# Four pairs of query tiles ahead instead of six, with attention's loads on SyncE and the statistics in one tile

## The chip, the cores and the metric

The kernel runs on one core of a Trainium2 chip. The core has TensorE (PE: matrix products into PSUM), VectorE (DVE), ScalarE (ACT), GpSimd (POOL) and SyncE (SP), which only issues transfers. Each engine works through its own list of instructions in order; they meet through semaphores. Sixteen DMA engines move data for all of them. SyncE's transfers go through a hardware queue (q1 in the profile), GpSimd's through a software queue (q0). The metric is the device time of one execution in microseconds, as the median of the runs.

## The reference

The kernel computes a decoder trunk of two layers over 1024 tokens of width 1024, in float32.

- Layer A is gated linear attention with four heads: projections of `x`, a recurrence in chunks, a gate, an output projection, and a layer norm on `ALPHA * x + y`.
- Layer B is attention in dilated windows over one shared K and V. Three groups of windows (width 128 step 1, 512 step 4, 2048 step 16) have their own queries and keys. There are eight query heads and two key heads, so four query heads share a key head.

```python
q, g = jnp.split(x @ w_in, [SWA_Q_TOTAL], axis=-1)
q = rope(q...) * SWA_HEAD_DIM ** -0.5
for gi, (window, dilation) in enumerate(SWA_GROUPS):
    o_g, lse_g = dilated_window_attention(q[:, :, gi], k_sh[:, :, gi], v_sh[:, :, gi], window, dilation)
wts = jax.nn.softmax(jnp.stack(lses, axis=0), axis=0)
o = jnp.sum(wts[..., None] * jnp.stack(outs, axis=0), axis=0)
return (o * jax.nn.silu(g)) @ w_out
```

The three groups' results are weighted by a softmax over the groups' log-sums. So for every token and head the minimum (the kernel works with negated scores) and the sum of the exponentials of all three groups have to meet before the outputs can be added.

## The kernel before, in words

**Products.** A float32 product is made from three products in the faster format `float32r`: a matrix is split into a high part (`wh`, `xh`) and the rest (`wl`, `xl`), and high x high, high x rest and rest x high are added up in PSUM. `project` makes 128 columns of a projection for all 1024 tokens: two halves of 512 tokens, eight steps, three products each, which is 48 matmuls of 512 columns (`acc<-x1h,wh` and its like). `load_w_now` loads the weight into `wf` (two buffers). With `added=True` ScalarE writes `wh` and the negated weight into `wl` (three buffers of each), and a GpSimd transfer adds the weight from memory onto `wl`.

**Pairs ahead.** `seven` makes two projections at once by Strassen's scheme: seven products of quarters in place of eight, 7 x 4 x 3 = 84 matmuls (`sev<-...`). `load_pair` fetches both weights (on SyncE) and forms the sums of quarters. The first three pairs are the keys; six more are query tiles, listed in `EARLY` as (unit, unit, group). The tiles wait in memory (`kd`, `qd`).

**Attention.** A unit is one query head. For `u` from 0 to 7 the loop in `layer_b` records `scores(u)`, `q_proj(u + 1)`, `attend(u)` and, for the first four units, `g_proj(u)`; the other gates come behind the loop.

- `q_proj` fetches a tile that is in `qd`, and projects the others.
- `scores` forms the scores (`lv<-K,Q`) of the groups 2, 1 and 0. VectorE adds the mask and takes the minimum, ScalarE takes the exponential and its sum. Both go into `sts`. The three groups order the tokens differently, so the statistics of groups 1 and 0 go through memory: `std<-sts` writes them, `nat<-std` gathers them in the order of group 2. From these VectorE and ScalarE form the factors `ew`; those of groups 0 and 1 go through memory again (`cwd<-ew`, `cw<-cwd`). All these small transfers are on SyncE.
- `attend` scales the probabilities `P` with the factors, turns them (`ms<-ident,P`), and multiplies with V (`po<-diag,V` for group 2, `po<-PT,V` for the others).
- `g_proj` is one more projection, with a tanh, that multiplies the unit's result `og`.

K and V of one key head are fetched by `reload_k` and `reload_v`. The second head's follow at `u == 3`. Weights (`wf`, `wl`), Q, K and V of attention are all issued by GpSimd.

**What sets the order.** The kernel records its operations, and a list scheduler (`Sched.order`) places them one by one, by the earliest start under a cost for each operation and then by the recorded rank. `later` changes the rank, `landing` adds to a transfer's cost. In the cost of before SyncE's and GpSimd's transfers don't slow each other. What the scheduler puts out is the fixed order of each engine's list. All operations are issued in one line of the code, so the profile's rows all bear that line's number (L454) and are told apart by the tiles.

## Time and profile before

| what | value |
|---|---|
| median of three runs | 1165.43 us (1163.35 to 1167.08) |
| the profiled execution | 1165.53 us |
| its span, from the first to the last instruction | 1163.8 us |
| mean granted clock of TensorE | 0.994 |
| PE busy | 1134.9 us |
| DVE, ACT, POOL busy | 833.9, 588.3, 212.2 us |
| transfers by SyncE's queue | 100.84 MB, 28.0% of 16 engines' span |
| transfers by GpSimd's queue | 39.85 MB, 14.5% |

A row of the view by stretches has the stretch, its length, then for each engine the busy time and the number of instructions, the granted clock of TensorE (1.00 is full speed), the share of the span that the DMA engines were busy, and GB/s. A row of a timeline has the start, the duration, the engine, the line, the operation with the tile written and the tiles read, and in brackets how long the engine stood idle before it and what ended that. A row of the chain of waits has start, duration, and what was waited for. A float32 product counts as two records of the matrix engine, a `float32r` product as one. Matmuls overlap, so rates are read from the distance of their starts.

### The profile page before, as it was taken

How to read it: one execution, taken by the hardware profiler on the slowest of the kernel's cores; microseconds unless marked ns; L12 is line 12 of the kernel's file. 1: busy time of each engine (PE TensorE's matmuls, PEld its weight loads, DVE VectorE, ACT ScalarE, POOL GpSimd, SP SyncE). 2: the span in 40 equal slices, each digit the busy share in tenths (PEclk: the TensorE clock that was granted, in tenths of full speed). 3: DMA queues.
4: the chain of work that ended last, by engine and by line, in shares of the span. 5: the costliest groups of instructions: out<-in, count | busy, mean ns of one | idle time of the engine just before them, and what ended most of it. 6: DMA issues, size and time to landing. Idle time of an engine off the chain costs nothing.

```text
span 1163.8 us, 20037 instructions
## 1 busy us (share of the span) xinstructions
PE 1134.9 (98%) x7672; PEld 956.7 (82%) x7672; DVE 833.9 (72%) x1712; ACT 588.3 (51%) x1175; POOL 212.2 (18%) x216
## 2 busy tenths in 40 slices
PE   9999999999999999999999999999987999999997
PEld 9888888889887888888888887888876888787876
DVE  6286952786967699887988966757645767686678
ACT  5355531635563335655656556455444555553343
POOL 1000000101122120122222343212222222132200
PEclk9999999999999999999999999999998999999999
DMA  7111223121144454855564695353453433351645
GB/s 267 57 39 37 74 81 96 60 73 39 56 170 138 136 188 156 268 164 135 138 162 137 173 282 124 83 119 75 74 169 78 101 74 75 84 151 42 191 135 181
DMA packets 103744, 141.97 MB, mean 122 GB/s; under 512 B 45312, under 2 KB 61568, under 8 KB 103648
## 3 DMA queue, kind: packets, MB, share of 16 engines
q1 hardware_dynamic: 90592, 100.84, 28.0%
q0 software_dynamic: 13056, 39.85, 14.5%
q8 instruction: 60, 0.98, 0.4%
q14 instruction: 36, 0.29, 0.1%
HBM read 111.11 MB, written 29.56 MB: 121 GB/s over the span
## 4 chain that ended last, share of the span: by engine, by line
PE 66%; DVE 14%; DMA 11%; ACT 4%; issue 3%; SPq 1%; POOL 0%; DVEq 0%; ACTq 0%
PE acc L454 36%; PE po L454 8%; PE vac L454 7%; PE lv L454 6%; DMA wf<-in_wB 3%; PE ms L454 3%; PE sev L454 3%; PE pro L454 2%; DMA std<-sts 2%; DVE wl L454 2%; DVE rt L454 2%; DMA nat<-std 2%; DVE P L454 2%; DMA wf<-in_wOB 2%; DVE sum L454 2%
## 5 line engine op out<-in xcount | busy, mean ns | idle before, releaser
L454 ACT ACTIVATE wh<-wf 128x1024 fp32r<-128x1024 f32 (+3 forms) x113 | 105.8, 938 | 126.0 <-PE acc L454 89.7
L454 PE MATMUL acc<-x1h,wh 128*128 128x512 f32 x320 | 138.8, 434 | 0.8 <-ACT t L454 0.7
L454 PE MATMUL acc<-x1h,wl 128*128 128x512 f32 x320 | 126.1, 394 | 0.0
L454 PE MATMUL acc<-x1l,wh 128*128 128x512 f32 x320 | 125.7, 393 | 0.0
L454 ACT ACTIVATE P<-P,sts 128x128 f32<-128x128 f32 (+2 forms) x192 | 81.4, 425 | 84.8 <-DVE sts L454 84.0
L454 DVE TENSOR_TENSOR wl<-wf,wh 128x1024 fp32r<-128x1024 f32 (+3 forms) x61 | 76.9, 1260 | 44.6 <-ACT wh L454 34.2
L454 PE MATMUL acc<-xh,wh 128*128 128x512 f32 x256 | 102.0, 398 | 0.0
L454 PE MATMUL acc<-xh,wl 128*128 128x512 f32 x256 | 99.8, 390 | 0.0
L454 PE MATMUL acc<-xl,wh 128*128 128x512 f32 x256 | 99.7, 390 | 0.0
L454 PE MATMUL sev<-T,wh 128*128 128x512 f32 x288 | 89.6, 392 | 0.8 <-ACT wh L454 0.4
L454 PE MATMUL lv<-K,Q 128*64 128x64 f32 (+2 forms) x512 | 72.3, 295 | 5.2 <-DMA Q<-qd 3.0
L454 PEld LDWEIGHTS acc<-x1h,wl 128*128 128x128 f32 x320 | 60.6, 189 | 13.5
L454 PEld LDWEIGHTS acc<-x1h,wh 128*128 128x128 f32 x320 | 61.1, 191 | 11.7 <-ACT t L454 1.6
L454 PEld LDWEIGHTS acc<-x1l,wh 128*128 128x128 f32 x320 | 61.0, 191 | 10.3
L454 PEld LDWEIGHTS lv<-K,Q 128*128 128x128 f32 (+1 forms) x512 | 53.4, 169 | 17.5 <-DVE sts L454 5.3
L454 PEld LDWEIGHTS sev<-T,wh 128*128 128x128 f32 x288 | 53.5, 188 | 14.2 <-ACT u L454 2.2
L454 POOL TENSOR_TENSOR wl<-wf,wh 128x1024 fp32r<-128x1024 f32 x9 | 21.5, 2386 | 231.5 <-PE ms L454 145.4
L454 DVE CUSTOM_DVE_ANT_0 P<-lv,bmask 128x256 f32<-128x256 f32 (+1 forms) x128 | 45.5, 376 | 21.0 <-PE lv L454 20.6
L454 PE MATMUL acc<-ogh,wh 128*128 128x512 f32 x152 | 60.1, 396 | 0.1
L454 PE MATMUL acc<-ogl,wh 128*128 128x512 f32 x152 | 59.3, 390 | 0.2 <-POOL ogl L454 0.2
L454 PE MATMUL acc<-ogh,wl 128*128 128x512 f32 x152 | 59.2, 389 | 0.0
L454 PE MATMUL sev<-T,wl 128*128 128x512 f32 x144 | 56.3, 391 | 0.9 <-DVE wl L454 0.9
(305 smaller groups left out, 2908.9 us busy)
## 6 DMA issues: line engine op xcount, KB each, us to landing
wf<-in_wA SPq DMA_DIRECT2D x24, 512.0 KB
wf<-in_wB POOLq DMA_DIRECT2D x20, 512.0 KB, 4.9
wl<-in_wB POOLq DMA_DIRECT2D x20, 512.0 KB, 8.0
wf<-in_wO SPq DMA_DIRECT2D x16, 512.0 KB
wf<-in_wOB SPq DMA_DIRECT2D x16, 512.0 KB
wf<-in_wV SPq DMA_DIRECT2D x12, 512.0 KB
wf<-in_wB SPq DMA_DIRECT2D x12, 512.0 KB
qd<-pair SPq DMA_DIRECT2D x12, 512.0 KB
```

Of the source, the lines that this page charges most:

```text
L454: getattr(handle[o.eng], meth)(*[conv(a) for a in args], **{k: conv(v) for k, v in kw.items()})
```

## The change

- `EARLY` holds four pairs, all of group 2, and no longer the two of group 1. So every unit now projects its queries of groups 0 and 1 in attention; for units 0, 2, 4 and 6 that is one projection more.
- The loads of `wf`, Q, K and V move from GpSimd to SyncE. The addition onto `wl` stays on GpSimd.
- `behind` makes a transfer depend on whoever wrote a given tile. The second head's K and V are put behind the write of the fourth unit's factors, `cwd[3]`.
- The gate `g_proj(u - 1)` is recorded behind `scores(u)` for u from 1 to 4, where `g_proj(u)` stood behind `attend(u)`.
- The statistics of group 2 are written directly into a third row of `nat`, which gets two buffers as `ew` does. So two reductions over three rows replace the pairwise minima and sums, and the group's factors are read from `ew` without a copy.
- The scheduler's cost puts all transfers on one common resource; GpSimd's cost 1.7 times as much.

```diff
-QUEUED, ISSUE = 5.2, 0.9
-EARLY = [(0, 1, 2), (2, 3, 2), (0, 2, 1), (4, 5, 2), (6, 7, 2), (4, 6, 1)]
+QUEUED, ISSUE, ADDED = 2.4, 0.9, 1.7
+EARLY = [(0, 1, 2), (2, 3, 2), (4, 5, 2), (6, 7, 2)]
...
+        behind = [v for v in self.trail if meth == "dma_start"]
...
-        o.reads += ins
+        o.reads += ins + behind
...
             if o.calls[0][0] == "dma_start":
-                queue[e] = max(queue[e], st) + c
-                o.t1 = st + c + QUEUED if e == "POOL" else queue[e] + 1.7
-                free[e] = st + (ISSUE if e == "POOL" else 0.37)
+                added = e == "POOL"
+                dma_free = max(dma_free, st + ISSUE * added) + c * (ADDED if added else 1.0)
+                o.t1 = dma_free + (QUEUED if added else 1.7)
+                free[e] = st + (ISSUE if added else 0.37)
...
-        (S.gpsimd if added else S.sync).dma_start(wf, src)
+        S.sync.dma_start(wf, src)
...
-                S.gpsimd.dma_start(K[c][g], kd[c][g])
+                S.sync.dma_start(K[c][g], kd[c][g])
...
-                    S.gpsimd.dma_start(Q[g], qd[u, g])
+                    S.sync.dma_start(Q[g], qd[u, g])
...
-            sts = hp.tile([128, 2, 24], F32, name="sts", bufs=2)
+            sts = hp.tile([128, 2, 16], F32, name="sts", bufs=2)
+            nat = hp.tile([128, 2, 3, 8], F32, name="nat", bufs=2)
...
+                        least, mass = (nat[:, i, 2, j:j + 1] if g == 2 else sts[:, i, col:col + 1] for i in range(2))
...
-            S.vector.tensor_tensor(mn, nat[:, 0, 0, :], nat[:, 0, 1, :], op=OP.min)
-            S.vector.tensor_tensor(mn, mn, sts[:, 0, 16:24], op=OP.min)
-            ew = hp.tile([128, 3, 8], F32, name="ew", bufs=1)
-            S.vector.tensor_sub(ew[:, 0:2], mn[:, None, :].to_broadcast([128, 2, 8]), nat[:, 0])
-            S.vector.tensor_sub(ew[:, 2], mn, sts[:, 0, 16:24])
+            S.vector.tensor_reduce(out=mn, in_=nat[:, 0].rearrange("p g n -> p n g"), op=OP.min, axis=AX.X)
+            ew = hp.tile([128, 3, 8], F32, name="ew", bufs=2)
+            S.vector.tensor_sub(ew, mn[:, None, :].to_broadcast([128, 3, 8]), nat[:, 0])
             S.scalar.activation(ew, ew, AF.Exp)
-            zz = hp.tile([128, 3, 8], F32, name="zz", bufs=1)
-            S.vector.tensor_mul(zz[:, 0:2], ew[:, 0:2], nat[:, 1])
-            S.vector.tensor_mul(zz[:, 2], ew[:, 2], sts[:, 1, 16:24])
-            zs = hp.tile([128, 8], F32, name="zs", bufs=1)
-            S.vector.tensor_add(zs, zz[:, 0, :], zz[:, 1, :])
-            S.vector.tensor_add(zs, zs, zz[:, 2, :])
+            S.vector.tensor_mul(nat[:, 1], ew, nat[:, 1])
+            S.vector.tensor_reduce(out=zs, in_=nat[:, 1].rearrange("p g n -> p n g"), op=OP.add, axis=AX.X)
             S.vector.reciprocal(zs, zs)
             S.vector.tensor_mul(ew, ew, zs[:, None, :].to_broadcast([128, 3, 8]))
-            cw = hp.tile([128, 24], F32, name="cw", bufs=1)
-            S.vector.tensor_copy(cw[:, 16:24], ew[:, 2, :])
...
             scores(u)
+            if 0 < u < 5:
+                g_proj(u - 1)
             if u == 3:
-                reload_k(1)
+                with S.behind(cwd[3]):
+                    reload_k(1)
             if u + 1 < 8:
                 q_proj(u + 1)
             if u < 7:
                 attend(u)
-                if u < 4:
-                    g_proj(u)
             if u == 3:
-                reload_v(1)
+                with S.behind(cwd[3]):
+                    reload_v(1)
```

The diff shows the table `EARLY` and the recorded ranks; the order that follows from them is seen in the engines' lists. SyncE's list, at the fourth unit's statistics (`std3`, `nat`) and factors (`cwd3`, `cw`), up to the fifth unit's, before:

```order
L454 DMA std3_8333<-sts_8193 128x2x4 x2
L454 DMA nat_8357<-std3_8333 64x1x8 x4
L454 DMA std3_8333<-sts_8193 8x16x8 x2
L454 DMA nat_8357<-std3_8333 64x8x1 x4
L454 DMA cwd3_8541<-ew_8483 8x8x8 x4
L454 DMA cw_8538<-cwd3_8541 128x8x1
L454 DMA cw_8538<-cwd3_8541 128x2x4
L454 DMA std4_8740<-sts_8513 128x2x4 x2
```

And with the change (`K12` is the second head's K of group 2, `qd42` the fifth unit's queries of group 2, `V12` the second head's V):

```order
L462 DMA nat_7833<-std3_8048 64x8x1 x4
L462 DMA wf_8182<-in_wB 128x1024
L462 DMA cwd3_8209<-ew_8195 8x8x8 x4
L462 DMA cw_8193<-cwd3_8209 128x8x1
L462 DMA cw_8193<-cwd3_8209 128x2x4
L462 DMA K12_8254<-kd12_5828 128x1024
L462 DMA wf_8259<-in_wB 128x1024
L462 DMA K11_8266<-kd11_5638 128x1024
L462 DMA K10_8278<-kd10_5469 128x1024
L462 DMA Q_8283<-qd42_6321 128x1024
L462 DMA V12_8287<-vd31_4625 64x1x512 x2
L462 DMA V11_8292<-vd_4634 128x4x128
```

Weights, K, Q and V now stand in SyncE's list, K and V behind the factors, and the fifth unit's statistics behind these.

PE's list at the fifth unit's first scores (`lv<-K12,Q`), before:

```order
L454 MATMUL acc_8470<-x1l1_4298,wh_8124 128x512
L454 MATMUL acc_8470<-x1h1_4269,wl_8136 128x512
L454 MATMUL lv_8489<-K12_8383,Q_8420 64x64 x16
L454 MATMUL lv_8510<-K11_8395,Q_8412 128x128
L454 MATMUL acc_8470<-x1h2_4311,wh_8124 128x512
L454 MATMUL acc_8470<-x1l2_4325,wh_8124 128x512
```

And with the change:

```order
L462 MATMUL po_8379<-PT_8393,V00_6526 128x128
L462 MATMUL po_8379<-PT_8415,V00_6526 128x128
L462 MATMUL lv_8442<-K12_8254,Q_8283 64x64 x16
L462 MATMUL lv_8461<-K11_8266,Q_8309 128x128
L462 MATMUL acc_8372<-x1h4_4366,wh_8069 128x512
L462 MATMUL acc_8372<-x1l4_4377,wh_8069 128x512
```

Before, the fifth unit's scores stood inside a query projection and ahead of the fourth unit's `attend`; now they stand behind the whole of it, and the projection around is a gate's.

More of the change, by code (lines that the diff above doesn't have):

```diff
@@ L14 @@
 OP = mybir.AluOpType
+AX = mybir.AxisListType
 T = 1024
@@ L216, in landing, with behind @@
         return _Landing(self, us)
+    def behind(self, *views):
+        return _Behind(self, views)
     def depend(self):
@@ L282, in order @@
         done = []
-        queue = {e: 0.0 for e in self.ENG}
+        dma_free = 0.0
         cur_set = None
@@ L503, in __exit__, with __init__, __enter__ @@
         self.s.least = 0.0
+class _Behind:
+    def __init__(self, s, views):
+        self.s, self.views = s, list(views)
+    def __enter__(self):
+        self.s.trail = self.views
+    def __exit__(self, *a):
+        self.s.trail = []
 class _Landing:
@@ L1403, in reload_v @@
             V[c][0] = page(p0, F32, f"V{c}0")
-            S.gpsimd.dma_start(V[c][0], vd0[c])
+            S.sync.dma_start(V[c][0], vd0[c])
         reload_k(0)
@@ L1483, in scores @@
                             out=px, in0=sc[:, o:o + nk], in1=mk, scale=-QSCALE, scalar=-LOWEST,
-                            op0=OP.add, op1=OP.min, accum_out=sts[:, 0, col:col + 1])
-                        S.scalar.activation(px, px, AF.Exp, scale=-1.0, bias=sts[:, 0, col:col + 1],
-                                             accum_out=sts[:, 1, col:col + 1])
+                            op0=OP.add, op1=OP.min, accum_out=least)
+                        S.scalar.activation(px, px, AF.Exp, scale=-1.0, bias=least, accum_out=mass)
                         o += nk
@@ L1495, in scores @@
             dst = std[u]
-            nat = hp.tile([128, 2, 2, 8], F32, name="nat", bufs=1)
             with S.landing(RUNS):
@@ L1511, in scores @@
                                           dst[0, s].rearrange("(i b p) -> i p b", i=2, b=8)[i])
[L1512 to L1524 removed]
+            cw = hp.tile([128, 16], F32, name="cw", bufs=1)
+            mn, zs = cw[:, 0:8], cw[:, 8:16]
+            S.vector.tensor_reduce(out=mn, in_=nat[:, 0].rearrange("p g n -> p n g"), op=OP.min, axis=AX.X)
+            ew = hp.tile([128, 3, 8], F32, name="ew", bufs=2)
+            S.vector.tensor_sub(ew, mn[:, None, :].to_broadcast([128, 3, 8]), nat[:, 0])
+            S.scalar.activation(ew, ew, AF.Exp)
+            S.vector.tensor_mul(nat[:, 1], ew, nat[:, 1])
+            S.vector.tensor_reduce(out=zs, in_=nat[:, 1].rearrange("p g n -> p n g"), op=OP.add, axis=AX.X)
             S.vector.reciprocal(zs, zs)
             S.vector.tensor_mul(ew, ew, zs[:, None, :].to_broadcast([128, 3, 8]))
[L1527 to L1528 removed]
             with S.landing(RUNS):
@@ L1537, in scores @@
                                   cwd[u][1].rearrange("(n p r) -> p n r", n=2, r=4))
-            U[u]["cw"] = cw
+            U[u]["cw"], U[u]["ew"] = cw, ew
         def attend(u):
@@ L1566, in attend @@
             x = P[2, 0][0].rearrange("p (j k q) -> p k j q", j=4, k=2)
-            w = cw[:, 16:24].rearrange("p (k j one) -> p k j one", k=2, j=4)
+            w = U[u]["ew"][:, 2].rearrange("p (k j one) -> p k j one", k=2, j=4)
             S.vector.tensor_mul(x, x, w.to_broadcast([128, 2, 4, 64]))
```

6 lines of the change are left out of this document (3 added, 3 removed).

## The prediction

> **What bounds the kernel now.** I read the shares of the engines first, then the engines' busy time in six stretches that I cut at the kernel's stages: layer A, the pairs of tiles ahead, attention's first three units with the scores of the fourth, the thirty microseconds after these, the rest of attention, and the output with its layer norm.
>
> ```profile
> span 1163.8 us, 20037 instructions
> PE 1134.9 (98%) x7672; PEld 956.7 (82%) x7672; DVE 833.9 (72%) x1712; ACT 588.3 (51%) x1175; POOL 212.2 (18%) x216
> core 0: us, PE busy (x) PEld busy (x) DVE busy (x) ACT busy (x) POOL busy (x), PEclk, DMA share, GB/s
> 0.00:510.00 510.00, 507.20 (x4327) 433.44 (x4328) 366.37 (x558) 246.65 (x355) 57.17 (x38) 1.00 0.35 115
> 510.00:682.00 172.00, 170.65 (x741) 138.33 (x741) 143.03 (x198) 102.54 (x173) 49.07 (x51) 1.00 0.60 161
> 682.00:860.00 178.00, 175.68 (x1030) 148.04 (x1030) 118.91 (x397) 99.84 (x286) 45.70 (x63) 1.00 0.47 109
> 860.00:890.00 30.00, 19.82 (x110) 16.34 (x109) 7.09 (x36) 8.20 (x27) 6.41 (x10) 0.83 0.68 186
> 890.00:1081.00 191.00, 186.34 (x1120) 158.23 (x1119) 136.34 (x433) 101.67 (x294) 47.91 (x52) 1.00 0.35 82
> 1081.00:1163.00 82.00, 75.18 (x351) 62.27 (x350) 62.20 (x94) 29.44 (x42) 5.92 (x3) 0.99 0.55 180
> ```
>
> TensorE sets the time: it is busy in every stretch but one. Attention (682 to 1081) leaves 2.3 + 10.2 + 4.7 = 17.2 us of it idle, and 10.2 of these lie in 30 us, at a granted clock of 0.83. PE's timeline and the chain of waits show that place, between the fourth unit's last scores and its turned probabilities:
>
> ```profile
> 857.65 1.02 PE L454 MATMUL lv<-K,Q 128*128 128x256 f32 x4
> 870.57 2.64 PE L454 MATMUL lv<-K,Q 128*64 128x64 f32 x34 [3.01 <-DMA Q<-qd]
> 883.63 1.08 PE L454 MATMUL ms<-ident,P 128*128 128x128 f32 x4 [7.17 <-DVE sts L454]
> ...
> 860.23 11.54 DMA std<-sts
> 873.12 8.22 DMA nat<-std
> ...
> 959.15 1.81 DMA std<-sts
> 962.31 5.12 DMA nat<-std
> ...
> 855.60 1.91 POOL L454 DMA_DIRECT2D K<-kd  x3
> 860.00:870.00 10.00, 7.56 (x34) 5.91 (x32) 1.13 (x2) 3.09 (x4) 2.36 (x4) 1.00 0.96 316
> ```
>
> Two waits, 3.01 and 7.17 us, have one cause: GpSimd issues the second head's K (855.60) and V just ahead of the fourth unit's statistics. The DMA engines are 96% busy, and the round trip of the statistics takes 11.54 + 8.22 = 19.8 us; in the sixth unit it takes 1.81 + 5.12 = 6.9 us. VectorE stands in order behind the late statistics, so PE's next evacuations wait too.
>
> The idle time is not the whole price. After it PE starts at a low clock:
>
> ```profile
> 884.37 0.78 PE L454 MATMUL acc<-x1h,wh 128*128 128x512 f32 x1
> 888.09 1.95 PE L454 MATMUL po<-diag,V 128*128 128x128 f32 x16
> 880.00:890.00 10.00, 6.37 (x30) 5.64 (x31) 4.68 (x28) 4.52 (x20) 0.00 (x0) 0.66 0.18 33
> 872.87 0.77 PE L454 MATMUL acc<-x1h,wh 128*128 128x512 f32 x1
> 920.33 1.50 PE lv L454 x34
> 682.47 16.32 PE acc L454 x72
> ```
>
> A 512-column matmul takes 16.32 / 72 = 0.2267 us warm. The nine from 884.37 to 888.09 took 3.72 where 2.04 is normal: 1.7 lost. The 34 score records from 870.57 to 872.87 took 2.30 where the sixth unit's take 1.50: 0.8 lost. The matmuls just behind them I put at 0.5. So this place costs 10.2 + 3.0 = **13.2 us**.
>
> **The change part by part.**
>
> *Two pairs fewer.* A pair by seven products is 7 x 4 x 3 = 84 matmuls, 19.0 us; two go, and four plain projections of 48 come, 10.9 us each, into attention. PE's order counts 756 rows of the pairs' product before and 588 after, 960 rows of projection before and 1152 after: 24 more, 24 x 0.2267 = **+5.4 us**. Nothing hides this, since the stretch of the pairs is 99% busy. ScalarE's and VectorE's share of the work moves along into attention, where they are busy 210 and 262 of 399 us; there is room.
>
> *K and V behind the fourth unit's factors.* K, Q and V now leave SyncE after the write of `cwd[3]`, so nothing large but weights can cross that unit's statistics. SyncE holds behind these waits only work of later units. What is late next? The fifth unit's scores. From the first turned tile of unit four to these PE has 36 projection matmuls (8.2 us), eight `po<-diag` (1.8), 16 turns and 27 `po<-PT`, at about 0.11 us a record and two records each (3.5 + 6.0): about 19 us. K in three parts, a weight and Q are 2.5 MB; at the 316 GB/s of the row above 8 us, at worst the 15 us that passed from 855.60 to 870.57. The factors' four writes take 2.5 us to issue and land some 3 us later:
>
> ```profile
> 882.58 2.48 SPq L454 DMA_DIRECT2D cwd<-ew  x4
> 1058.67 3.08 DMA cwd<-ew
> ```
>
>  So it needs 13 to 20 us, of 19 and the lead that the next part gives: a wait of 0 to 3 us; I take under 1, as no statistics or V go along now.
>
> *Gates one unit later, two projections for every unit.* What PE has between a unit's last score and its own turn is now, by PE's order, 54, 81, 72, 75, 63, 60, 57 and 72 projection matmuls, and the next unit's scores: 14 to 24 us, shortest in the first (14.8) and the fifth unit (14.3). What the statistics need, from the units where PE waited at the end of it:
>
> ```profile
> 808.38 0.59 PE L454 MATMUL lv<-K,Q 128*128 128x256 f32 x2
> 822.63 0.63 PE L454 MATMUL ms<-ident,P 128*128 128x128 f32 x4 [0.69 <-DVE P L454]
> 957.34 0.61 PE L454 MATMUL lv<-K,Q 128*128 128x256 f32 x2
> 969.63 0.66 PE L454 MATMUL ms<-ident,P 128*128 128x128 f32 x4 [0.35 <-DVE P L454]
> 1042.23 0.59 PE L454 MATMUL lv<-K,Q 128*128 128x256 f32 x2
> 1059.13 0.63 PE L454 MATMUL ms<-ident,P 128*128 128x128 f32 x4 [0.61 <-DVE P L454]
> ```
>
> 13.7, 11.7 and, in the last unit, where VectorE has the output's splits to do as well, 16.3 us. The fourth unit has 17.0 where it had 13.5, so its 13.2 us go, unless the two reasons below bring part back.
>
> *Loads from GpSimd to SyncE.* Weights, Q, K and V now stand in SyncE's queue among the statistics, each issue about 0.35 us there, and a weight's issue waits for ScalarE to free its buffer. By the order that buffer was freed a projection earlier at every unit, so this wait should be over. A 512 KB load ahead of a small transfer costs it 0 (they were in flight before too, on the other queue) to 0.5 MB / 316 GB/s = 1.7 us. There are one or two per unit: 0 to 3.4 us, on cover of 14 to 24. I take 1.5, nearest to the 5.45 us below, which a weight and Q in flight gave a round trip that else takes 1.81:
>
> ```profile
> 768.32 5.45 DMA std<-sts
> 775.79 2.22 DMA nat<-std
> ```
>
> That is hidden except in units one and five.
>
> *Statistics in one tile.* Eleven VectorE instructions of a unit become six. At the 0.17 us of the row below five fewer are 0.9 us of the chain; a strided reduction over 24 elements may give some back (0.17 to 0.3 for the two). PE waited on this chain for 0.69 + 0.35 + 0.61 us in all: gain 0 to 1.6.
>
> ```profile
> 879.06 0.17 DVE L454 TENSOR_TENSOR ew<-mnB,nat 128x16 f32<-128x16 f32 x1
> PE lv L454 <- DVE sts L454: 1.9, 5, 0.7
> PE po L454 <- DVE PT L454: 1.6, 3, 0.6
> ```
>
> *The sum.* Without the fourth unit attention has 17.2 - 10.2 = 7.0 us idle. The scores' own waits (1.9) and the turned tiles' (1.6) stay, with the short gaps; of the rest I take 2 as gone, the new waits counted. 1163.8 + 5.4 - 13.2 - 2.0 = 1154.0. The profiled run took 1165.53, 1.7 more than its span, and stands 0.1 above the median, so **1155.6 us**.
>
> **The rivals.**
>
> *Nothing waits any more* (0.14). The cover removes another 3 us: 1152.5. For it speaks that all gaps but the fourth unit's are under 0.7; against it that scores wait on VectorE by their own rhythm.
>
> *One queue* (0.14). The statistics get through only behind the loads ahead of them: 3.4 us each, of which 3 show in unit one, 3 in unit five and under 1 in two others, no cold start: +5, 1160.5. Against it: a separate queue did not save the fourth unit either (11.54). The Trainium skill's page "DMA: Bandwidth & Descriptors", section "Queues, rings and completion order", speaks for it: each DMA engine alternates packet by packet between queues, but takes one queue's descriptors in the order of its ring. By that rule small transfers lose their turn with this change. The last unit shows the nearest case, with the output's weight on the statistics' own queue:
>
> ```profile
> 1044.95 0.41 SPq L454 DMA_DIRECT2D wf<-in_wOB  x1
> 1046.17 2.74 DMA nat<-std
> ```
>
> 2.74 us for the gather behind it, between the 2.22 and the 5.12 above; so the rule's cost is small as far as a row shows it, and the rival stays below the forecast.
>
> *K comes too late* (0.08). 15 us from issue, as in the old collision, and no lead: 3 us of wait and perhaps 1.7 of cold start, 1160.
>
> *Slower: bulk ahead of the statistics twice* (0.07; once, 0.07). In SyncE's order the first head's V stands right ahead of the first unit's statistics, and the second head's V ahead of the fifth's: the two units with the least cover. If SyncE reaches them late, what happened in unit four happens there: a chain of 24.9 us (858.7 to 883.6) against 14.5, 10.4 of wait and 1.7 of cold clock, 12 us each. It decides when V (1.5 MB, 5 us) is still in flight as the last scores are done. Once: 1167.7, no change; twice: 1180. Against it: by PE's order there are 17 to 20 us of scores and projections between these loads and the last statistics.
>
> **How the numbers follow.** Forecast 0.50 (1155.6), and the cases above. About 0.3%, 3.5 us, is what a measurement here can tell from no change; so faster means under 1162. The forecast, the first rival and most of the second and third are faster: 0.50 + 0.14 + 0.11 + 0.06 = 0.81. Within: the rest of these and the single collision, 0.12. Slower: the double one, 0.07. The range goes from 1149.5 (no idle time left in attention would be 1163.8 + 5.4 - 13.2 - 7.0 + 1.7 = 1150.7, and a microsecond for the output) to 1164, which leaves out the collisions.
>
> **What would show it.** PE's idle time in attention falls from 17.2 to about 5 us, with no stretch under a clock of 0.95; the pairs' stretch ends some 38 us earlier and attention is about 30 us longer. The fourth unit's `std<-sts` and `nat<-std` take 10 us together or less, and no PE row has a wait above 1.5 us. Wrong would be a wait for `K`, `Q` or `V` at the fifth unit's first scores, a VectorE wait on `nat<-std` over 10 us in unit one or five, or PE waiting for `wl`. If the span falls by 13 or more, the 5.4 us were hidden, and PE was not the bound that I take it for.

## The result and the profile after

The changed kernel takes **1146.26 us** (1145.40 to 1147.29) where the kernel before takes 1164.39: a ratio of 0.9843, with a 95% interval of 0.982 to 0.9867. Forecast were 1155.6, with a range from 1149.5: the side is right, the gain of 18 us is about twice the forecast one, and the time lies 3 us below the range. The page of the changed kernel, and its stretches cut at the same stages (pairs, attention, output):

```profile
span 1143.6 us, 20006 instructions
PE 1129.4 (99%) x7696; PEld 959.8 (84%) x7696; DVE 813.4 (71%) x1634; ACT 583.9 (51%) x1165; POOL 181.7 (16%) x168
504.00:640.00 136.00, 134.98 (x595) 110.70 (x594) 113.92 (x158) 82.57 (x140) 39.20 (x36) 1.00 0.62 168
640.00:1055.00 415.00, 411.23 (x2418) 351.18 (x2417) 275.55 (x832) 228.65 (x636) 85.56 (x94) 1.00 0.45 103
1055.00:1143.00 88.00, 81.42 (x382) 68.20 (x380) 62.48 (x96) 29.43 (x42) 1.29 (x1) 0.98 0.50 167
```

PE runs 24 instructions more and the span is 20.2 us shorter. Attention leaves PE 3.8 us idle where it left 17.2, at a clock of 1.00. What is left, in PE's view of who waited for whom:

```profile
PE po L462 <- DVE diag L462: 1.0, 1, 1.0
PE acc L462 <- ACT t L462: 1.0, 1, 1.0
PE lv L462 <- DVE sts L462: 0.8, 2, 0.5
PE ms L462 <- DVE P L462: 0.4, 1, 0.4
PE po L462 <- DVE PT L462: 0.3, 1, 0.3
```

The fourth unit, where before lost 13 us, in SyncE's and VectorE's timelines:

```profile
826.05 1.23 SPq L462 DMA_DIRECT2D std<-sts  x2
830.31 2.68 SPq L462 DMA_DIRECT2D nat<-std  x4
...
842.58 1.00 SPq L462 DMA_DIRECT2D cw<-cwd  x2
843.68 0.42 SPq L462 DMA_DIRECT2D K<-kd  x1
...
835.61 0.18 DVE L462 TENSOR_TENSOR ew<-cw,nat 128x24 f32<-128x24 f32 x1
```

The last write of the statistics goes out at 826.7, and 8.9 us later VectorE forms the factors; before it took 18.8. K's issue stands behind the gather `cw<-cwd`. All of this is as the prediction described it. The gain does not need it, though, as the experiments show.

**Where the 20.2 us lie.** I cut both traces at the same two instructions: the first `acc<-x1h` behind the pairs, and the first matmul of the output (`acc<-woh,ogh`). First the pairs' matmuls, then all work of attention, of the kernel before:

```profile
505.71:682.30 176.59, 174.83 (x756) 140.97 (x756) 29.60 (x44) 21.13 (x36) 1.00 0.60 162
682.30:1110.53 428.23, 411.07 (x2386) 346.83 (x2385) 280.13 (x883) 217.75 (x614) 104.66 (x126) 0.99 0.45 111
```

and of the changed one:

```profile
504.77:640.26 135.49, 134.47 (x588) 109.94 (x588) 23.26 (x34) 16.41 (x28) 1.00 0.63 169
640.26:1091.44 451.18, 447.41 (x2578) 381.18 (x2576) 293.57 (x852) 237.37 (x644) 85.53 (x94) 1.00 0.46 110
```

- Pairs: 41.1 us less (foretold: 38). The 168 matmuls that went are 38.1. Of the other 3.0 the rows show 0.7 as idle time (176.59 - 174.83 = 1.76 before, 135.49 - 134.47 = 1.02 after); 2.3 are in no row.
- Attention: 22.95 us more (foretold: about 30). 192 projection matmuls came, 43.5 us; 13.4 us of idle time went, 3.0 of cold clock by the prediction's rows, and 4.2 that again no row shows (PE's busy time rose by 36.3, not by 43.5 less 3.0).
- The rest, 2 us: 0.9 in layer A, whose order is the same in both, and 1.1 in the output.

How waits can stand in no row (2.3 + 4.2 = 6.5 us here) is seen in any run of matmuls of the changed kernel:

```profile
832.01 0.39 PE L462 MATMUL acc<-x1h,wl 128*128 128x512 f32 x1
832.24 0.39 PE L462 MATMUL acc<-x1h,wh 128*128 128x512 f32 x1
```

A record lasts 0.39 us and the next one starts after 0.23. A wait below 0.16 us leaves no idle time at all, and a longer one shows shortened by that much. In the pairs, where all matmuls are alike, the distance of starts shows the lost time. In attention the 4.2 us are the rest of a sum that takes the cold clock at the prediction's 3.0; that they are short waits is a reading and not shown.

### The profile page after: what moved, and what is told of

Same layout as the page of the kernel before. It is cut to its first block, busy times and chain, and to the rows that moved or that the text cites. A ratio compares the mean times of both kernels' runs of the same rounds, so it can differ in the third digit from the quotient of the medians.

```text
span 1143.6 us, 20006 instructions
## 1 busy us (share of the span) xinstructions
PE 1129.4 (99%) x7696; PEld 959.8 (84%) x7696; DVE 813.4 (71%) x1634; ACT 583.9 (51%) x1165; POOL 181.7 (16%) x168
## 4 chain that ended last, share of the span: by engine, by line
PE 89%; DVE 7%; ACT 1%; DMA 1%; issue 1%; SPq 0%; DVEq 0%; ACTq 0%
PE acc L462 47%; PE sev L462 11%; PE lv L462 9%; PE po L462 9%; PE vac L462 7%; PE ms L462 4%; PE pro L462 2%; DVE rt L462 2%; DVE wl L462 1%; DMA nat<-std 1%; DVE x1l L462 1%; DVE t L462 1%; DVE P L462 1%; ACT t L462 0%; DVE Q L462 0%
## 5 line engine op out<-in xcount | busy, mean ns | idle before, releaser
L462 PE MATMUL acc<-x1h,wh 128*128 128x512 f32 x384 | 165.6, 431 | 1.0 <-ACT t L462 1.0
L462 PE MATMUL acc<-x1h,wl 128*128 128x512 f32 x384 | 150.6, 392 | 0.0
L462 PE MATMUL acc<-x1l,wh 128*128 128x512 f32 x384 | 150.0, 391 | 0.0
L462 ACT ACTIVATE P<-P,sts 128x256 f32<-128x256 f32 (+1 forms) x128 | 59.9, 469 | 65.9 <-DVE sts L462 65.3
L462 PEld LDWEIGHTS acc<-x1h,wl 128*128 128x128 f32 x384 | 72.1, 188 | 15.9
L462 PEld LDWEIGHTS acc<-x1h,wh 128*128 128x128 f32 x384 | 72.6, 189 | 13.0 <-ACT t L462 1.2
L462 PEld LDWEIGHTS acc<-x1l,wh 128*128 128x128 f32 x384 | 72.6, 189 | 12.0
L462 PE MATMUL sev<-T,wh 128*128 128x512 f32 x224 | 69.3, 391 | 0.1
L462 POOL DMA_DIRECT2D wl<-in_wB x36 | 31.8, 903 | 225.6 <-ACT wl L462 177.3
L462 DVE TENSOR_TENSOR t<-t,sinT 128x512 f32<-128x512 f32 x46 | 34.4, 748 | 33.7 <-ACT t L462 33.6
```

Of the source, the lines that this page charges most:

```text
L462: getattr(handle[o.eng], meth)(*[conv(a) for a in args], **{k: conv(v) for k, v in kw.items()})
```

## The experiments

Times stand against the kernel before on the same chip. "Gap" is the stretch from the issue of the fourth unit's last statistics to PE's turn of its probabilities (`ms<-ident,P`): its length, the projection matmuls in it by PE's records of `acc`, and PE's idle time there.

| run | us | ratio (95%) | gap us | `acc` | idle us |
|---|---|---|---|---|---|
| before | 1164.4 | 1 | 23.4 | 45 | 10.2 |
| changed | 1146.3 | 0.984 (0.982-0.987) | 15.8 | 71 | 0 |
| e1 old price | 1155.0 | 0.991 (0.989-0.994) | 16.4 | 74 | 0 |
| e2 GpSimd issues | 1157.4 | 0.994 (0.991-0.996) | 12.9 | 58 | 0 |
| e3 no dependence | 1144.4 | 0.982 (0.980-0.985) | 26.4 | 106 | 0 |
| e4 six pairs | 1153.5 | 0.990 (0.988-0.992) | 13.9 | 55 | 1.4 |
| e7 gates as before | 1162.2 | 0.998 (0.996-0.999) | 19.3 | 33 | 12.0 |
| e12 old statistics | 1146.2 | 0.983 (0.981-0.985) | 15.8 | 71 | 0 |
| e5 before + four pairs | 1163.6 | 1.000 (0.998-1.001) | 20.1 | 58 | 7.1 |
| e6 before + dependence | 1179.6 | 1.013 (1.011-1.015) | 10.1 | 27 | 4.1 |
| e9 before + gates | 1162.2 | 0.997 (0.996-0.998) | 19.2 | 43 | 8.0 |
| e10 neither dependence nor gates | 1144.0 | 0.981 (0.979-0.983) | 25.2 | 101 | 0 |

### The terms of the prediction, one by one

**e3: without the dependence.**

```diff
-                with S.behind(cwd[3]):
-                    reload_k(1)
+                reload_k(1)
...
-                with S.behind(cwd[3]):
-                    reload_v(1)
+                reload_v(1)
```

> The changed kernel without the dependence of the second head's K and V on the fourth unit's factors; all else as changed. My theory: K and V go out ahead of the fourth unit's statistics again, their round trip goes from under 10 us to 15 to 20, and as the unit has 17 us of cover where it had 13.5, 3 to 8 us of PE's wait come back, with 1 to 3 us of cold clock: 1150 to 1156. Rival: on SyncE the loads stand behind the waits for their pages and the weights and do not cross the statistics, or the cover is enough: within 1.5 us of the changed kernel, 1145 to 1147.5.

1144.35 us: not slower, and just under what the rival expected. The collision is back: the statistics take 23.6 us. But PE has no idle time in the gap. The view by stretches, for the rows of `acc` alone (length of the gap, then busy time and records on PE, on its weight load, on VectorE and ScalarE; clock, share of the DMA engines, GB/s):

```profile
826.90:853.30 26.40, 24.61 (x106) 19.46 (x104) 2.97 (x5) 5.34 (x9) 1.00 0.80 184
860.20:883.60 23.40, 10.96 (x45) 8.44 (x43) 1.37 (x2) 1.18 (x2) 0.87 0.83 235
```

The second row is the kernel before. The same late statistics, 106 projection matmuls in the gap against 45. So the term of 13.2 us had the right size and the wrong cause: what decides is what PE has to do meanwhile.

**e6: the dependence alone, in the kernel before.**

```diff
             if u == 3:
-                reload_k(1)
+                with S.behind(cwd[3]):
+                    reload_k(1)
...
             if u == 3:
-                reload_v(1)
+                with S.behind(cwd[3]):
+                    reload_v(1)
```

> The kernel before with one part of the change: the second head's K and V behind the fourth unit's factors, still issued by GpSimd, six pairs ahead. My prediction's term: the fourth unit's 13.2 us (10.2 idle, 3.0 of cold clock) go, its round trip falls from 18.8 us to 9 or less, and K is waited for under 1 us: 1151 to 1153. Rival: with so little cover the transfers that now come later are waited for in the fifth unit, or cross its statistics instead, 5 to 10 us: 1156 to 1161. Against the term as a cause in the changed kernel stands the run without the dependence (the round trip took 23.6 us there, and PE waited 2.1): this run tells what the dependence is worth alone.

(The 2.1 us that the text names lie in a later unit.) 1179.6 us, **15 us slower**, beyond both expectations. The dependence does what it says: the statistics take 6.9 us. PE's timeline of that run:

```profile
869.47 1.09 PE L460 MATMUL ms<-ident,P 128*128 128x128 f32 x4 [4.07 <-DVE P L460]
872.49 3.62 PE L460 MATMUL po<-diag,V 128*128 128x128 f32 x16 [1.94 <-DVE diag L460]
878.07 0.50 PE L460 MATMUL acc<-x1h,wh 128*128 128x512 f32 x1 [1.96 <-DVE sg L460]
886.75 1.97 PE L460 MATMUL ms<-ident,P 128*128 128x128 f32 x8 [3.37 <-ACT P L460]
```

These are 11.3 us of idle time in place of 10.2. The fifth unit's scores used to stand in the gap; they need K, and K now comes behind the factors. 27 projection matmuls (6 us) are left for a gap of 10. The next units get fewer too, and PE's other idle time in attention rises from 7.0 to 15.0 us, in waits of up to 3.9. The rest of the loss shows in no row as idle time. The prediction asked "what is late next" and looked at K's arrival; it did not look at what leaves the gap.

**e7: the changed kernel with the gates as before.**

```diff
             scores(u)
-            if 0 < u < 5:
-                g_proj(u - 1)
...
                 attend(u)
+                if u < 4:
+                    g_proj(u)
```

> The changed kernel with one thing undone: the output gates of the first four units are written down at their old place, behind each unit's own output, not one unit later; four pairs, SyncE, price and statistics as changed. If only the amount of projection work in attention counts, since the planner places it where it has need: within 2 us of the changed kernel, 1144.5 to 1148.5. If its place counts (a projection written one unit later is what stands ready when the statistics travel): PE's idle in attention goes from 3.8 to 8 us or more and the time to 1150 to 1156.

1162.2 us, slower than both expectations: 16 of the 18 us are gone. Here the dependence stands without the gates that fill its gap: 33 projection matmuls in the gap, 12.0 us idle, cold clock behind it. This run shows something more, in the chain of waits:

```profile
834.19 6.54 DMA std<-sts
...
840.79 2.22 DMA nat<-std
...
844.79 0.34 SPq L462
...
845.18 7.89 DMA nat<-std
...
854.93 1.10 PE ms L462 x4
...
845.18 0.89 POOL L462 DMA_DIRECT2D wl<-in_wB  x1 [10.60 <-ACT wl L462]
```

The piece of 0.34 us at 844.79 is SyncE's issue of a 512 KB weight. The gather issued right behind it takes 7.89 us where the one ahead took 2.22. (The weight itself was issued only as ScalarE was done with its buffer, at 844.78, and the gather stood behind it in SyncE's list.) The Trainium skill's page "DMA: Bandwidth & Descriptors", section "Queues, rings and completion order", says that a DMA engine takes one queue's descriptors in the order of its ring. These rows fit it, and it is the mechanism of my rival "one queue". They do not show it alone, since GpSimd issued another 512 KB, the addition onto `wl`, at the same moment (the last row). A late gather costs nothing where the gap is full.

**e10: neither the dependence nor the moved gates** (the edits of e3 and e7 together).

```diff
-            if 0 < u < 5:
-                g_proj(u - 1)
...
-                with S.behind(cwd[3]):
-                    reload_k(1)
+                reload_k(1)
```

> The changed kernel with two things undone together: gates at their old place, and no dependence of the second head's K and V. With the gates alone undone the fourth unit had 31 projection matmuls and waited 12 us, since the fifth unit's scores could not start before K. If the dependence is what takes that cover away: without it the scores and two more projections stand there again, the wait falls to 3 us or less, 1147 to 1152. If the collision is the worse of the two: the stall of the kernel before (10 us idle, 3 cold) comes back, 1158 to 1163.

1143.98 us: 2.2 below the changed kernel, and below what was expected of either theory. So the moved gates make up for what the dependence takes away, and the two together gain nothing. In the gap SyncE even issues V between the gathers:

```profile
836.21 0.60 SPq L462 DMA_DIRECT2D std<-sts  x1
836.90 1.34 SPq L462 DMA_DIRECT2D Q<-qd  x1
838.33 2.68 SPq L462 DMA_DIRECT2D V<-vd  x4
841.05 1.51 SPq L462 DMA_DIRECT2D nat<-std  x2
845.14 0.34 SPq L462 DMA_DIRECT2D wf<-in_wB  x1
845.53 1.84 SPq L462 DMA_DIRECT2D V<-vd  x3
847.41 3.17 SPq L462 DMA_DIRECT2D nat<-std  x2
```

21.6 us pass until the factors, and PE fills them with 101 projection matmuls and the fifth unit's scores. This is also the fastest version measured, though 0.2% is less than what tells two of these kernels apart.

**e9 and e11: the moved gates in the kernel before, alone and with the dependence.**

```diff
             scores(u)
+            if 0 < u < 5:
+                g_proj(u - 1)
...
                 attend(u)
-                if u < 4:
-                    g_proj(u)
```

> The kernel before with one part of the change: the first four output gates are written down one unit later. Cover theory (what counts is the projection work that PE has between a unit's last scores and its own turn): the fourth unit gets up to 48 matmuls, 10.9 us, beside the 43 that it has; its 10.2 us of idle time and the cold clock behind it go although its round trip stays at 18 us or more: 1149 to 1154. My prediction's account (the crossing loads are the cause, the cover only a part): the statistics are still late, and since VectorE stands in order behind them half of the stall stays: 1157 to 1161.

> The kernel before with two parts: gates one unit later, and the second head's K and V behind the fourth unit's factors. The dependence alone cost 15 us. Cover theory: the gate takes the place of the fifth unit's scores in the fourth unit's gap, so most of these 15 us go, but no gain over the gates alone is left: 1152 to 1160, and not below the run with the gates alone. If the dependence does gain once the gap is filled: 3 us or more below that run.

1162.2 and 1163.7 us (e11: 0.999, 0.997 to 1.001), so both expectations for e9 miss, and e11 lies above its own too. Recorded one unit later, the gate still does not get into the gap: 43 projection matmuls (45 in the kernel before), 8.0 us idle. The scheduler spends it elsewhere. A recorded place is only a rank.

In e11 the gates do make up for the dependence (1179.6 to 1163.7), but no gain is left. K, issued by GpSimd, is let go by the factors' write and meets the factors' second half. GpSimd's timeline, the chain of waits, and PE:

```profile
864.26 1.91 POOL L460 DMA_DIRECT2D K<-kd  x3
```

```profile
867.17 12.34 DMA cw<-cwd
...
1018.08 3.65 DMA cw<-cwd
```

```profile
881.03 2.07 PE L460 MATMUL ms<-ident,P 128*128 128x128 f32 x8 [8.21 <-DVE P L460]
```

12.34 us for a gather that takes 3.65 later on. The collision has only moved from `nat` to `cw`. On SyncE, K's issue stands behind that gather (the changed kernel's rows above). A separate queue protected nothing here.

**e12: the statistics as before.**

```diff
-            S.vector.tensor_reduce(out=mn, in_=nat[:, 0].rearrange("p g n -> p n g"), op=OP.min, axis=AX.X)
+            S.vector.tensor_tensor(mn, nat[:, 0, 0, :], nat[:, 0, 1, :], op=OP.min)
+            S.vector.tensor_tensor(mn, mn, sts[:, 0, 16:24], op=OP.min)
...
```

> The changed kernel with one thing undone: the statistics as before, eleven VectorE instructions in three small tiles instead of six in one. My prediction's term was 0 to 1.6 us. If the chain of statistics is covered everywhere, as the changed kernel's rows say (no wait on it over 0.5 us): 1146 to 1148. If the order that the planner makes with the longer chain costs cover: 1150 or more.

1146.15 us, 0.1 away from the changed kernel: the lower end of the term. PE hardly waits for that chain any more.

### What is left: pairs, place of issue, price

**e4: six pairs in the changed kernel; e5: four pairs in the kernel before.**

```diff
-EARLY = [(0, 1, 2), (2, 3, 2), (4, 5, 2), (6, 7, 2)]
+EARLY = [(0, 1, 2), (2, 3, 2), (0, 2, 1), (4, 5, 2), (6, 7, 2), (4, 6, 1)]
```

(e4; e5 is the same line the other way round.)

> The changed kernel with six pairs ahead as before: 24 matmuls of 0.2267 us fewer, and attention has four projections less to put between the units. My prediction's step (5.4 us that nothing hides) gives 1146.3 - 5.4 = 1140.9 if the other parts don't need the moved projections as cover. Rival (cover): the projections that stand in attention are what hides the statistics; with fewer, 5 us or more of waits come back, some of them not shown as idle: 1146 to 1152, PE's idle in attention 8 us or more instead of 3.8.

> The kernel before with one part of the change: four pairs of query tiles ahead instead of six. The step of my prediction: 24 matmuls more that nothing hides, the fourth unit's stall as it was: 1164.4 + 5.4 = 1169.8. Cover theory, which the run with six pairs suggests (there six pairs instead of four cost 7 us in the changed kernel): the four projections that now stand in attention hide waits that the records show as idle time (17.2 us in attention) and some that they don't, so 1155 to 1159, with PE's idle in attention at 8 us or less although K and V still go out ahead of the fourth unit's statistics.

With 24 matmuls fewer, e4 is 7.3 us slower. The matmuls save 5.4, so 12.7 us are lost elsewhere: PE's idle time in attention grows from 3.8 to 11.4 us, and the other 5 show in no row. The longest waits:

```profile
PE ms L462 <- DVE P L462: 3.0, 2, 1.7
PE lv L462 <- DVE sts L462: 2.1, 3, 1.1
PE acc L462 <- DVE sg L462: 2.0, 1, 2.0
```

In e5 neither expectation holds: the time does not change. The four projections pay back their 5.4 us but not more, and the stall is still there, 7.1 us with 58 projection matmuls in the gap.

**e1: the old price in the changed kernel.**

```diff
-                added = e == "POOL"
-                dma_free = max(dma_free, st + ISSUE * added) + c * (ADDED if added else 1.0)
-                o.t1 = dma_free + (QUEUED if added else 1.7)
+                queue[e] = max(queue[e], st) + c
+                o.t1 = st + c + QUEUED if e == "POOL" else queue[e] + 1.7
...
```

> The changed kernel with one thing undone: the planner prices DMAs as before (a queue of its own for each engine, 5.2 us for a GpSimd load) instead of one common resource. The order then differs from the first pair on. My theory: of the 20.2 us of span the change gave, 8 (3 in the pairs, 5 in attention) were waits of a fraction of a microsecond that the records show as busy, and the order made with the common price took them away. Then the pairs cost 19.3 to 19.6 us each again instead of 19.04 (2 us for seven) and attention about 5 more: 1153 us. Rival, that the loads' new queue took them away: the loads are still on SyncE, so the pairs' order may differ but no time comes back: 1146 to 1148.

1155.0 us, as the order theory said, and in the places that it named. In the profiled execution, which took 1159.1, the pairs take 5 us more, 1.78 of them in one wait for ScalarE's evacuation, and attention 9 more. PE's longest waits there are 4.8 us before turned probabilities and 4.2 for Q, where the changed kernel has 0.4 and none:

```profile
574.72 0.73 PE L461 MATMUL sev<-T,wh 128*128 128x512 f32 x2 [1.78 <-ACT u L461]
```

```profile
PE ms L461 <- DVE P L461: 4.8, 2, 3.2
PE lv L461 <- DMA Q<-qd: 4.2, 3, 1.9
```

**e2 and e8: GpSimd issues weights, Q, K and V in the changed kernel, with the new price and with the old.**

```diff
-        S.sync.dma_start(wf, src)
+        (S.gpsimd if added else S.sync).dma_start(wf, src)
...
-                S.sync.dma_start(K[c][g], kd[c][g])
+                S.gpsimd.dma_start(K[c][g], kd[c][g])
...
```

(e8 with the edit of e1 beside it.)

> The changed kernel with one thing undone: projection weights, Q, K and V are issued by GpSimd again (K and V of the second head still behind the fourth unit's factors). The order is the same up to the end of the pairs. My theory (the order by the common price gave the 8 us; SyncE itself gives nothing): pairs at 19.04 us, attention within 1.5 us, in all 1146 to 1148. Rival (loads off GpSimd's queue gave the 5 us in attention): 1151 to 1152, with the loss in attention only. Third possibility, against the rule I weighed in the prediction: a separate queue for bulk is better for the statistics, 1143 to 1145.

> The changed kernel with two things undone together: weights, Q, K and V issued by GpSimd, and the planner's price of DMAs as before. It tells apart why the run with GpSimd alone was 11 us slower than the changed kernel. If the new price (1.7 times the transfer for a GpSimd load) was the wrong one for GpSimd, the old one mends it: 1146 to 1150, and the statistics' round trips, 14 to 22 us in five units there, are under 10 us again. If GpSimd's issue itself lets large loads cross the statistics: 1155 to 1160 again, round trips of 12 us and more in several units.

1157.4 us, and 1167.4 with the old price (1.003, 1.000 to 1.005). Both are slower than all that was expected. In e2 the pairs are undisturbed, and the 13 us by which its span is longer are lost in attention, 7.2 of them as idle time. In e8 the stall is the one of e11: GpSimd's K crosses the factors' second half, and PE waits 8.77 us for scaled probabilities (863.89). So the place of issue is worth 11 us in this kernel (12 with the old price, e1 against e8), where I had charged it with a cost that is hidden.

**e13 to e17: the three parts, each with and without.** Together with before, e5 and e10 these fill the table (no dependence, gates as before). The four kernels e10, e15, e16 and e17 have the new statistics, the others the old; in the changed kernel that was worth 0.1 us.

```diff
# e13: the kernel before, new price
-                queue[e] = max(queue[e], st) + c
+                dma_free = max(dma_free, st + ISSUE * added) + c * (ADDED if added else 1.0)
# e14: the kernel before, SyncE
-                S.gpsimd.dma_start(K[c][g], kd[c][g])
+                S.sync.dma_start(K[c][g], kd[c][g])
# e15, e16, e17: e10 with six pairs; with GpSimd; with the old price (edits of e4, e2, e1)
```

> The kernel before with the new price of DMAs only; six pairs, loads by GpSimd. Planning theory: with a price under which all transfers share one resource the planner sees that K and V delay the fourth unit's statistics and keeps projections for that gap, as in the run with neither dependence nor moved gates, where 99 projection matmuls stood in the gap and PE did not wait though the round trip took 21.6 us. Then PE's wait there falls from 10.2 us to 3 or less: 1150 to 1156, even with six pairs, and the pairs cost 19.04 us each (3 us). Queue theory: with the loads on GpSimd the order on the chip is not the planned one, and the stall stays whatever it plans: 1161 to 1170.

> The kernel before with weights, Q, K and V on SyncE only; old price, six pairs. Under the old price each issuing engine has a queue of its own, so loads on SyncE's queue delay the statistics in the plan too. Planning theory: the planner now sees the collision, and the fourth unit's wait falls to 3 us or less: 1150 to 1156. If the place of issue is nothing without the new price: 1161 to 1166. If the loads hold the statistics up on SyncE (my third rival): slower than 1168.

(The third rival of that text is the prediction's "one queue".)

> Price and SyncE, six pairs (the changed kernel without dependence, moved gates and the two pairs fewer). The changed kernel with six pairs took 1153.5, with 11.5 us of idle time in attention against 3.8. Cover theory: the same here, 1149 to 1155, since four projections fewer stand in attention. If the shortage there came of the dependence (it takes the fifth unit's scores from the gap), 5.4 us fewer matmuls pay here: 1138 to 1143.

> Price and four pairs, loads by GpSimd (the changed kernel without dependence and moved gates, and with the loads on GpSimd). Planning theory: the plan has 90 or more projection matmuls in the fourth unit's gap, and PE waits 3 us or less there: 1146 to 1152. Queue theory: GpSimd's loads cross other units' statistics, as in the run with GpSimd and the dependence (round trips of 14 to 22 us in five units, 1157.4): 1155 to 1162.

> Four pairs and SyncE, price as before (the changed kernel without dependence, moved gates and new price). Supply theory: with the four more projections in attention there is enough to put into the fourth unit's gap, and the old price sees a collision on SyncE's own queue, so the wait there is 3 us or less; the pairs cost 19.3 to 19.6 us each (2 to 5 us in all), as in the other runs with the old price: 1147 to 1154. Price theory: without the new price the gap gets about 45 projection matmuls, PE waits 7 us or more, and with the cold clock and the pairs' loss it is 1157 to 1163.

| | GpSimd, old price | GpSimd, new price | SyncE, old price | SyncE, new price |
|---|---|---|---|---|
| six pairs | 1164.4, 1 | 1187.6, 1.019 (e13) | 1162.1, 0.996 (e14) | 1160.7, 0.996 (e15) |
| four pairs | 1163.6, 1.000 (e5) | 1168.3, 1.002 (e16) | 1150.1, 0.986 (e17) | 1144.0, 0.981 (e10) |

No part alone gains more than 0.4%. Four pairs and SyncE together gain 1.4%, with the new price 1.9%; no interval reaches more than 0.3% to either side. Of the expectations, only e17's supply theory and the second one of e14 give the measured time; e13, e15 and e16 came out slower than all that was expected. The pair that tells most is e5 and e17. The two differ in the place of issue and in the statistics' form. e5's gap, then e17's:

```profile
844.10:864.20 20.10, 12.96 (x58) 10.37 (x56) 1.64 (x3) 2.95 (x5) 0.92 0.85 219
```

```profile
839.80:862.50 22.70, 21.41 (x94) 17.11 (x92) 2.75 (x4) 3.54 (x6) 1.00 0.94 229
```

In both the transfers are in each other's way: the DMA engines are 85 and 94% busy, and the statistics take 16.2 and 19.4 us. With the loads on SyncE the scheduler keeps 94 projection matmuls for that gap, not 58, and PE does not wait. Why it does so I read from its cost and have not measured: by the old price GpSimd's loads and SyncE's small transfers don't slow each other, so the planned gap is short; put on SyncE they stand in one queue, and the plan knows that the statistics come late.

Six pairs with the same knowledge (e15) have 40 projection matmuls in the gap, and PE waits:

```profile
863.10:887.80 24.70, 9.98 (x40) 6.78 (x38) 2.07 (x3) 0.28 (x1) 0.95 0.66 150
```

```profile
887.75 1.12 PE L462 MATMUL ms<-ident,P 128*128 128x128 f32 x4 [5.80 <-DVE P L462]
```

In e14 (six pairs on SyncE, old price) PE waits only 1.32 us at the fourth unit's turn, as that run's planning theory said. But then nothing is left for the fifth unit's turn, and the run gains only 0.4%:

```profile
897.85 1.97 PE L454 MATMUL ms<-ident,P 128*128 128x128 f32 x8 [6.35 <-ACT P L454]
```

So two things are needed, work that can be put into the gap and a plan that puts it there. The new price's part beside that: in the pairs, seven take 138.95 us in e17 and 135.69 in e10, and the same 3 us are the difference to the kernel before. All runs with the new price have pairs of 19.04 to 19.15 us behind the first; all with the old one have some of 19.4 to 22.8.

Only in part is it known why the new price with GpSimd's loads is so bad (e13). PE waits 32.9 us in attention there, most of it in the first, second, fourth and fifth units. The plan holds projections back in some gaps and has none in the next; in e16 too, 11.40 us in the fifth unit behind a fourth with some 140 projection matmuls. In e13's fourth unit the order of SyncE's list is to blame as well. Its statistics were last written at 876.7, but the last gathers stand in the list behind writes of the fifth unit's statistics, which have to wait for that unit's scores. SyncE's and PE's timelines:

```profile
901.72 5.52 SPq L455 DMA_DIRECT2D std<-sts  x3
907.29 0.59 SPq L455 DMA_DIRECT2D nat<-std  x1
...
913.03 1.11 PE L455 MATMUL ms<-ident,P 128*128 128x128 f32 x4 [6.91 <-DVE P L455]
```

Why the plan puts them so stays open.

**e18: a fifth pair on e10.**

```diff
-EARLY = [(0, 1, 2), (2, 3, 2), (4, 5, 2), (6, 7, 2)]
+EARLY = [(0, 1, 2), (2, 3, 2), (0, 2, 1), (4, 5, 2), (6, 7, 2)]
```

> The changed kernel with neither dependence nor moved gates (1144.0), and with a fifth pair ahead, the second projection of the first and third unit: 12 matmuls of 0.2267 us fewer. The first unit's projection stands ahead of all statistics and hides nothing; the third unit's stands in the second unit's gap. If the supply left is enough: 1144.0 - 2.7 = 1141.3, PE's idle in attention 4 us or less. If each unit of supply is needed, as the run with six pairs says: 1146 to 1152, with waits of 3 us or more in the second to fourth unit.

1152.9 us (0.989, 0.987 to 0.991), 9 slower than e10, for 12 matmuls fewer. The place was not the second to fourth unit, though. The fourth unit's gap is 33.9 us long and full (124 records of `acc`), and then there is nothing left for the fifth unit's turn:

```profile
881.63 1.97 PE L462 MATMUL ms<-ident,P 128*128 128x128 f32 x8 [7.32 <-ACT P L462]
```

## Why the prediction was right and wrong

- **What bounds the kernel.** Right: PE, now 99% busy with more instructions. "If the span falls by 13 or more, the 5.4 us were hidden, and PE was not the bound": it fell by 20.2, and PE is the bound. The sentence forgot that added work can pay by filling waits, and that some waits look like work.
- **Two pairs fewer, +5.4, "Nothing hides this, since the stretch of the pairs is 99% busy".** This is the step that failed. As a count of matmuls it holds. As a term of the sum it does not: the four projections are the supply from which attention's gaps are filled, and with six pairs in place of four the changed kernel is 7.3 us slower, not 5.4 faster (e4). I costed the added matmuls and put their worth as filler at nothing. And "99% busy" was not full: 3 us went from the pairs beside the matmuls, as the new price changed their order. The sum also put the price at nothing, without a reason, although the diff shows it; it is worth 6 us between e17 and e10, 8.8 in the changed kernel (e1).
- **The fourth unit's stall, -13.2.** It went, and the rows of the changed kernel read as foretold (8.9 us for the round trip, no wait above 1.04, no clock under 0.95). The cause was wrong. The dependence alone costs 15 us (e6), and without it and the gates the kernel is as fast (e10). All signs that I had named were signs of the stall's end and none of its cause. As the forecast gain rested on this term, the right side was in part luck.
- **Gates one unit later, cover of 17.0 for 13.5.** The figure of the cover was near (15.8 us of full work). I took the gates for a help to the dependence. They are what it needs in order not to cost time: without them 16 us are lost (e7).
- **Loads to SyncE, 1.5 us, hidden.** Wrong in sign, 11 us in the changed kernel (e2). The collisions that the rival feared take place (7.89 us behind a weight in e7), but the place of issue gives more than they cost, as far as the runs tell by the plan that reckons with one queue.
- **Statistics, 0 to 1.6; other idle time, -2.0.** 0.1 (e12), and 3.2 of the 7.0 us in all.
- **The sum.** By place, of the 10.4 us of span that were missed (1154.0 against 1143.6) 6.5 show in no row, 1.9 are more idle time gone than the sum had (1.2 in attention, 0.7 in the pairs), and 2 lie in layer A and the output. The stall was no miss in size: 10.2 of the 13.4 us of idle time that went are its own, with the cold clock behind them.
- **The rivals.** "Nothing waits any more" (1152.5) named the right state and still lay 6 us too high, since it counted idle time only. The collisions on SyncE do take place (e3, e10), inside full gaps.

## What to carry to other kernels

A stall on a late result is removed by making the result earlier or by having other work at that place. Before a dependence is added, list what stands in the gap today and ask which of it the dependence takes away. Work that a cheaper algorithm could take out of a stage may be worth more as filler: count the supply of movable work against the gaps, unit by unit. And where a scheduler sets the order, its price of a resource is a part of the change like any other: a wait that it does not know of is a wait that it does not fill.

## What the runs showed that I had not expected

- Waits of PE under some 0.16 us show as busy time: 2.3 us in the pairs, and perhaps the 4.2 in attention. They are found by the distance of starts (756 matmuls in 176.59 us are 0.2336 each, 588 in 135.49 are 0.2304, and the first pair of each takes 2 us more than the others), not by the idle column.
- Small gathers suffer from large loads on another queue (12.34 us for 3.65, K from GpSimd) as well as behind one on their own (7.89 for 2.22 behind a weight, with another load from GpSimd at the same time). In the changed kernel the order of issue keeps K out of the gather's way; e10 shows that a full gap does as well.
- Parts that gain little or nothing one by one (0.4%, nothing, and a loss of 1.9%) gain 1.9% together. Undoing one of them at a time in the changed kernel gives 16, 11, 9, 7 and -2 us, which add up to far more than the 18 there are.
